# A two-layer hybrid encoder on one core: shift and scale rows summed together, x loaded through ScalarE's queue, and other buffers for the raw value weights, the lambda vectors and the bias table

## The chip, the cores and the metric

The kernel runs on one core of one Trainium2 chip. The metric is the device time of one execution in microseconds (us). The kernel is one program with one instruction stream for each engine: TensorE (PE in the profile), VectorE (DVE), ScalarE (ACT), GpSimd (POOL) and SyncE (SP). SP issues nearly all DMAs. The order of the instructions of each engine is fixed when the kernel is built; at run time an engine only waits, by semaphores, for what its next instruction needs.

## What is computed

Two layers, each with 512 tokens and 1024 channels in float32. Cut to what matters here:

```python
c_act = silu(c)
for l in range(2):
    shift, scale, gate = split(c_act @ w_ada[l] + b_ada[l])      # three rows of 1024
    h = rms_norm(x, g_pre[l]) * (1 + scale) + shift
    (cq, ckv, kr, za, qb, kb, vb, zb, qc, kc, vc, zc, gcols) = split_cols(h @ w_in[l])
    o_a = (mla_branch(cq, ckv, kr, ...) * silu(za)) @ w_o_mla[l]             # 8 heads
    o_b = (swa_branch(qb, kb, vb, sink[l], swa_bias) * silu(zb)) @ w_o_swa[l] # window 128, T5 bias
    lam = exp(sum(lam_q1 * lam_k1)) - exp(sum(lam_q2 * lam_k2)) + lam_init
    o_c = (diff_branch(qc, kc, vc, lam, g_sub, rel_bias) * silu(zc)) @ w_o_diff[l]
    g = sigmoid(gcols)                                            # 3 x 1024 gate columns
    y = (g[0] * o_a + g[1] * o_b + g[2] * o_c) @ w_out[l]
    x = x + gate * rms_norm(y, g_post[l])
```

The T5 bias of the windowed and the differential branch comes from a table of 32 x 12 numbers, spread over relative positions with a one-hot matrix.

## The kernel before

**Arithmetic.** Activations lie with channels on the partitions and tokens along the row ("hT", 8 tiles of 128 x 512). Nearly every product is made of three matmuls on a high and a low part of both operands (function `mm3`; L87, L88 and L89 are its three matmuls). So each raw weight tile is split first: ACT copies it to the high part (L81), DVE subtracts to get the low part (L84; POOL in a few places). One projection unit (`wunit`) takes one raw tile of 128 x 1024 ("wr") to "wh" and "wl" and then runs 24 matmuls of 512 columns into one tile of PSUM.

**Buffers.** A tile has a tag, and the tiles of a tag take its buffers in turn, in the order in which the program makes them. A tile waits until the tile that had its buffer before is done with. In SBUF: "wr" 2, "wh" 3, "wl" 3, "big" 8, "op" 12, "u" 8, "o" 4, "p" 2, "pt" 6, "tf" 2, "ta" 2. In PSUM: "dn" 2, "sc" 2, "tr" 2, "pj" 1, "av" 1. A waiting instruction holds up all that stand behind it on its engine.

**Order.** The tile framework orders the instructions of each engine when the kernel is built, by a simulated timeline with priorities (`tc.high_priority`) and with explicit "not before" relations (`behind`, `fence`). A tile that gets its buffer late in the program's order is therefore also placed late, and so is every tile behind it in the same tag's turn.

**Layer 0's start (`layer0_input`, L339).** `mod_load` (L143) brings columns of w_ada, `mod_chunk` (L187) makes from them one or two of the eight 128-wide pieces of shift and scale: DVE adds up eight 128 x 128 or 128 x 256 products for the shift and eight for the scale (L203, L206), PE sums over the partitions by a product with ones (L212), and DVE writes "ashf" and "amul" (L215 to L220). There are five chunks, for j = 0, 1, 2-3, 4-5 and 6-7; the scale of j = 1 is summed by PE itself (L194). `normed` scales the four tiles of x, PE transposes them into eight PSUM tiles (L346), ACT applies amul and ashf (L363) and makes the high part of hT, DVE the low part. For each j PE then adds the MLA input products (128 x 416, PSUM sc, sc, pj, av) and three tiles of za (128 x 512, PSUM dn, dn, tr). SP issues the loads of x behind those of the first chunk.

**After it (`rest_of_layer`, L1072).** The fourth tile of za ("z3"), norms and rotary parts (`mla_inputs`), the values (`mla_v`, L642), and the eight MLA heads (`mla_attention`), of which each has four score tiles (ps_sc), a maximum of each on DVE (L770), an exponential on ACT (L771), a scaling on POOL (L775), sixteen 128 x 128 transposes on PE (L704, ps_tr) and the product with the values (L713 to L717, ps_av). Then the program has `setup_bias` (L428): two matmuls (L438) of the one-hot matrix ("oh") into "dn" tiles, copied to "bt" and stored. Then the gate projections (`gates_early`), which take "dn" tiles too, the windowed branch, the differential branch and the merges. `setup_small` (L404) loads rotary tables and the lambda vectors and reduces the latter.

Of the kernel before, what the change touches and what calls it, by code (L numbers as in the profile page):

```python
# [50 lines left out]
def hybrid_kernel(ctx, tc, x, c, w_ada, b_ada, g_pre, g_post, w_in, g_q, w_uq, g_kv, w_ukv,  # L51
# [91 lines left out]
    def mod_load(l, j, n, tags):  # L143
        tags = iter(tags)
        res = []
        for which in range(2):
            raws = [T(next(tags), [P, KT // n, n * P]) for _ in range(n)]
            for i, raw in enumerate(raws):
                loads.append(sp.dma_start(out=raw, in_=w_ada[l].rearrange("(p k) b -> p k b", k=KT)
                             [:, i * (KT // n):(i + 1) * (KT // n),  # L150
                              which * D + j * P:which * D + (j + n) * P]))
            res.append([raws[k * n // KT][:, k % (KT // n)] for k in range(KT)])
# [12 lines left out]
    for t in range(NT):  # L165
        sp.dma_start(out=xt0[t], in_=x[t * P:(t + 1) * P, :])
# [20 lines left out]
    def mod_chunk(l, j, n, srcs, on_pe):  # L187
        pst = Q("tr")
        accs = []
        for which in range(2):  # L190
            src = srcs[which]
            if which in on_pe:
                for k in range(KT):
                    pe.matmul(pst[:, which * n:which * n + 1], src[k], cact[:, k:k + 1],  # L194
                              start=k == 0, stop=k == KT - 1)
                continue
            acc = T("o", [P, S])[:, 0:n * P]
            accs.append((which, src, acc))
        for k in range(KT):
            for which, src, acc in accs:  # L200
                with behind(*(stts if k < 4 else amuls)[-1:]) if stts else nullcontext():
                    if k == 0:
                        end = dve.tensor_scalar(out=acc, in0=src[0], scalar1=cact[:, 0:1],  # L203
                                                scalar2=None, op0=ALU.mult)
                    else:
                        end = dve.scalar_tensor_tensor(out=acc, in0=src[k],  # L206
                                                       scalar=cact[:, k:k + 1], in1=acc,
                                                       op0=ALU.mult, op1=ALU.add)
        stts.append(end)
        for which, src, acc in accs:  # L210
            for i in range(n):
                mm = pe.matmul(pst[:, which * n + i:which * n + i + 1],  # L212
                               acc[:, i * P:(i + 1) * P], ones[:, 0:1], start=True, stop=True)
        js = slice(j, j + n)
        dve.tensor_tensor(out=ashf[l][:, js], in0=pst[:, 0:n],  # L215
                          in1=par(l, PR_SHIFT, j, n), op=ALU.add)
        dve.scalar_tensor_tensor(out=amul[l][:, js], in0=pst[:, n:2 * n], scalar=1.0,
                                 in1=par(l, PR_SCALE, j, n),
                                 op0=ALU.add, op1=ALU.add)
        end = dve.tensor_tensor(out=amul[l][:, js], in0=amul[l][:, js],  # L220
                          in1=par(l, PR_GPRE, j, n), op=ALU.mult)
        sums.append(mm)
        amuls.append(end)
# [106 lines left out]
    def new_hT():  # L330
# [3 lines left out]
    AT = {0: (0,), 1: (1,), 2: (2,), 4: (3,)}  # L334
    CH = [(1, 1, ("wh", "wl"), (1,)),
          (2, 2, ("wh", "wl", "big", "big"), ()), (4, 2, ("big",) * 4, ()),
          (6, 2, ("big",) * 4, ())]

    def layer0_input():  # L339
        hh, hl = new_hT()  # L340
        mod_chunk(0, 0, 1, src0, ())
        xn = [normed(xt0[t]) for t in range(NT)]
        trs = [Q(g) for g in ("sc", "sc", "pj", "av", "dn", "dn", "tr", "tr")]
        for t in range(NT):
            for j in range(KT):
                pe.transpose(trs[j][:, t * P:(t + 1) * P], xn[t][:, j * P:(j + 1) * P], ident)  # L346
        xT = [T("op", [P, S]) for _ in range(KT)]
        for j in range(1, KT):
            act_copy(xT[j], trs[j])
        acc = acc4(True)  # L350
        zp = [Q("dn"), Q("dn"), Q("tr")]
        ws = mla_in_weights(0)
        for j in range(KT):
            w = next(ws)
            zr = T("tf", [P, S])[:, 0:ZK * P]
            zh = T("pt", [P, S], F32R)
            zl = T("pt", [P, S], F32R)
            sp.dma_start(out=zr, in_=w_in[0][j * P:(j + 1) * P, C_ZA:C_ZA + ZK * P])
            act_copy(zh[:, 0:ZK * P], zr)
            sub(zl[:, 0:ZK * P], zr, f(zh[:, 0:ZK * P]), pool)  # L360
            for i in AT.get(j, ()):
                mod_chunk(0, *CH[i][0:2], mod_load(0, *CH[i][0:3]), CH[i][3])
            act.activation(out=xT[j], in_=xT[j] if j else trs[0], func=AF.Identity,  # L363
                           scale=amul[0][:, j:j + 1], bias=ashf[0][:, j:j + 1])
            act_copy(hh[:, j], xT[j])
            sub(hl[:, j], xT[j], f(hh[:, j]))
# [61 lines left out]
    def setup_bias():  # L428
        oh = T("wr", [P, 1024])
# [5 lines left out]
        bt = T("wr", [P, 1024])  # L435
# [206 lines left out]
    def mla_v(l, cl):  # L642
        raw = T("wr", [P, 1024])
        h = T("wh", [P, 1024], F32R)
        sp.dma_start(out=raw, in_=w_ukv[l])
        rv = raw.rearrange("p (h b) -> p h b", h=8)[:, :, 64:128]
        hv = h[:, 0:512].rearrange("p (h b) -> p h b", h=8)
        lv = h[:, 512:1024].rearrange("p (h b) -> p h b", h=8)
        with behind():
            act_copy(hv, rv, par(l, PR_GKV))  # L650
            dve.scalar_tensor_tensor(out=lv, in0=rv, scalar=par(l, PR_GKV), in1=f(hv),
                                     op0=ALU.mult, op1=ALU.subtract)
# [417 lines left out]
    def rest_of_layer(l, hh, hl, acc, za):  # L1070
# [21 lines left out]
        if l == 0:  # L1092
            fence[:] = [amuls[2]]
# [45 lines left out]
        mb = merge_steps(l, 1, w_o_swa, ub, hh, hl, m, None)  # L1139
        od = diff_attention(l, hh, hl, lambda n: [next(mb) for _ in range(n)])  # L1140
# [79 lines left out]
```

## Time and profile before

| | |
|---|---|
| time, median of 3 | 1180.55 us (1180.5 to 1180.76) |
| the profiled execution's own time | 1178.78 us |
| its span | 1176.7 us |
| TensorE busy | 1146.0 us, 97% |
| VectorE busy | 844.2 us, 72% |
| ScalarE busy | 631.5 us, 54% |
| GpSimd busy | 181.3 us, 15% |
| mean granted TensorE clock | 0.993 |

The profile is of one execution. Its times count from the start of the span. "Busy" counts an instruction from its start to its end, and since instructions of one engine overlap in its pipeline, the distance between the starts of two neighbours (the step) is often shorter than the duration of one. In a timeline a row has the start, the duration, engine, line, operation, tiles, and in brackets the idle time ahead of it with what ended it. In a table of windows "(x)" counts instructions, PEclk is the clock that TensorE was granted, 1.00 being full.

### The profile page before, as it was taken

Reading aid. Unit: us, or ns where it says so; the run is one execution under the profiler, and the core shown is the slowest. Engines: PE = TensorE matmul, PEld = TensorE weight load, DVE = VectorE, ACT = ScalarE, POOL = GpSimd, SP = SyncE. Lnnn points to the kernel's source line nnn. Section 1 sums busy time; section 2 is a strip of 40 time slices with the busy share of each in tenths; the row PEclk is TensorE's granted clock in tenths of the full one; section 3 lists DMA queues with packets and bytes.
Section 4 is the critical chain, followed back from the end, with each engine's and each line's share of the span. In section 5 each row is a group of like instructions: output and inputs, shape, how many; then the busy total and the mean of one; then the engine's idle time right before and its main releaser. Section 6 shows DMA issues by size and latency. Waiting matters only on the chain.

```text
span 1176.7 us, 15536 instructions
## 1 busy us (share of the span) xinstructions
PE 1146.0 (97%) x5428; PEld 946.0 (80%) x5428; DVE 844.2 (72%) x1754; ACT 631.5 (54%) x1250; POOL 181.3 (15%) x226
## 2 busy tenths in 40 slices
PE   5899999999999999999999999999999999999997
PEld 4768788878887888888888888888888888888886
DVE  7956686898866687876577567688786568786654
ACT  5355464655543457664357456565564346675432
POOL 4310212122210010101211011222121001100120
PEclk9899999999999999999999999999999999999999
DMA  9537532256355433433454432324533333334442
GB/s 340 190 92 217 186 106 76 72 145 186 108 141 164 110 81 87 117 107 126 143 184 135 114 108 75 86 52 123 157 97 92 95 95 96 88 99 115 136 159 92
DMA packets 169522, 146.86 MB, mean 125 GB/s; under 512 B 7679, under 2 KB 146999, under 8 KB 169444
## 3 DMA queue, kind: packets, MB, share of 16 engines
q1 hardware_dynamic: 166148, 140.08, 40.9%
q10 hardware_dynamic: 3168, 5.77, 1.3%
q8 instruction: 43, 0.70, 0.2%
q14 instruction: 35, 0.29, 0.1%
q0 software_dynamic: 128, 0.01, 0.0%
HBM read 135.83 MB, written 14.20 MB: 127 GB/s over the span
## 4 chain that ended last, share of the span: by engine, by line
PE 84%; DVE 6%; DMA 3%; issue 3%; ACT 1%; POOL 1%; SPq 0%; DVEq 0%; POOLq 0%; ACTq 0%
PE ps_dn L87 20%; PE ps_dn L89 20%; PE ps_dn L88 19%; PE ps_tr L704 5%; PE ps_sc L89 2%; PE ps_sc L87 2%; PE ps_sc L88 2%; PE ps_av L714 1%; PE ps_av L713 1%; PE ps_sc L952 1%; PE ps_sc L953 1%; DMA wr<-in_w_in 1%; DVE o L206 1%; PE ps_pj L87 1%; PE ps_pj L88 1%
## 5 line engine op out<-in xcount | busy, mean ns | idle before, releaser
L87 PE MATMUL ps_dn<-hTh,wh 128*128 128x512 f32 x840 | 331.8, 395 | 1.4 <-DVE zz L479 0.8
L89 PE MATMUL ps_dn<-hTh,wl 128*128 128x512 f32 x840 | 330.5, 393 | 0.4 <-DVE wl L84 0.4
L88 PE MATMUL ps_dn<-hTl,wh 128*128 128x512 f32 x840 | 330.1, 393 | 0.0
L84 DVE TENSOR_TENSOR wl<-wr,wh 128x1024 fp32r<-128x1024 f32 x141 | 178.9, 1269 | 98.5 <-ACT wh L81 97.5
L81 ACT ACTIVATE wh<-wr 128x1024 fp32r<-128x1024 f32 x141 | 149.1, 1058 | 162.7 <-PE ps_dn L88 111.2
L87 PEld LDWEIGHTS ps_dn<-hTh,wh 128*128 128x128 f32 x840 | 158.2, 188 | 33.2 <-PE ps_dn L89 1.0
L89 PEld LDWEIGHTS ps_dn<-hTh,wl 128*128 128x128 f32 x840 | 158.0, 188 | 33.3 <-DVE wl L84 0.9
L88 PEld LDWEIGHTS ps_dn<-hTl,wh 128*128 128x128 f32 x840 | 158.1, 188 | 31.7
L84 DVE TENSOR_TENSOR pt<-ps_tr,pt 128x512 fp32r<-128x512 f32 x136 | 92.2, 684 | 30.5 <-ACT pt L81 29.6
L81 ACT ACTIVATE pt<-ps_tr 128x512 fp32r<-128x512 f32 x136 | 78.8, 596 | 64.8 <-PE ps_tr L704 63.6
L775 POOL TENSOR_SCALAR p<-p,st 128x512 f32<-128x512 f32 x64 | 52.2, 834 | 279.3 <-DVE st L773 243.7
L704 PE MATMUL ps_tr<-ident,p 128*128 128x128 f32 x544 | 92.4, 273 | 0.9 <-POOL p L775 0.6
L704 PEld LDWEIGHTS ps_tr<-ident,p 128*128 128x128 f32 x544 | 69.5, 141 | 20.2 <-POOL p L775 1.8
L87 PE MATMUL ps_dn<-u,wh 128*128 128x512 f32 x192 | 75.9, 395 | 0.0
L89 PE MATMUL ps_dn<-u,wl 128*128 128x512 f32 x192 | 75.9, 395 | 0.0
L88 PE MATMUL ps_dn<-u,wh 128*128 128x512 f32 x192 | 75.2, 391 | 0.0
L963 POOL TENSOR_SCALAR ta<-ta,st 128x512 f32<-128x512 f32 x32 | 26.7, 834 | 306.9 <-ACT wh L81 143.1
L894 POOL TENSOR_SCALAR p<-p,st 128x256 f32<-128x256 f32 (+1 forms) x64 | 42.1, 676 | 157.7 <-DVE st L892 130.4
L771 ACT ACTIVATE p<-ps_sc,st 128x512 f32<-128x512 f32 x64 | 43.7, 685 | 28.0 <-DVE st L770 27.7
L770 DVE TENSOR_REDUCE st<-ps_sc 128x1 f32<-128x512 f32 x64 | 43.4, 686 | 21.3 <-PE ps_sc L89 20.8
L886 ACT ACTIVATE p<-p,st 128x256 f32<-128x256 f32 (+1 forms) x64 | 35.7, 558 | 21.9 <-DVE st L884 21.2
L959 ACT ACTIVATE p<-p,st 128x512 f32<-128x512 f32 x32 | 23.1, 723 | 38.8 <-DVE st L957 38.7
(345 smaller groups left out, 2100.5 us busy)
## 6 DMA issues: line engine op xcount, KB each, us to landing
wr<-in_w_in SPq DMA_DIRECT2D x105, 512.0 KB, 3.7
wr<-in_w_ada SPq DMA_DIRECT2D x32, 512.0 KB, 3.6
wr<-in_w_out SPq DMA_DIRECT2D x16, 512.0 KB, 3.6
big<-in_w_ada SPq DMA_DIRECT2D x10, 512.0 KB, 7.6
big<-in_x SPq DMA_DIRECT2D x8, 512.0 KB, 5.3
wr<-in_w_o_mla SPq DMA_DIRECT2D x8, 512.0 KB, 4.0
wr<-in_w_o_swa SPq DMA_DIRECT2D x8, 512.0 KB, 3.4
wr<-in_w_o_diff SPq DMA_DIRECT2D x8, 512.0 KB, 3.7
```

The costliest lines, as they stand in the source:

```text
L81: return act.activation(out=out_, in_=in_, func=AF.Copy, scale=scale)
L84: return (eng or dve).tensor_tensor(out=out_, in0=a, in1=b, op=ALU.subtract)
L87: pe.matmul(o, ah, bh, start=start, stop=False)
L88: pe.matmul(o, ah, bl, start=False, stop=False)
L89: pe.matmul(o, al, bh, start=False, stop=stop)
L704: pe.transpose(tr[:, i * P:(i + 1) * P], b, ident)
L770: dve.tensor_reduce(out=nm[:, t:t + 1], in_=s, axis=AX.X, op=ALU.max, negate=True)
L771: act.activation(out=pr[:, t], in_=s, func=AF.Exp, bias=nm[:, t:t + 1], accum_out=sm[:, t:t + 1])
L775: pool.tensor_scalar(out=pr[:, t], in0=pr[:, t], scalar1=rr[:, t:t + 1], scalar2=1.0, op0=ALU.mult, op1=ALU.mult)
L886: act.activation(out=pr[:, i, :w], in_=pr[:, i, :w], func=AF.Exp, bias=nm[:, i:i + 1], accum_out=sm[:, i:i + 1])
L894: pool.tensor_scalar(out=pr[:, i, :w], in0=pr[:, i, :w], scalar1=rr[:, i:i + 1], scalar2=1.0, op0=ALU.mult, op1=ALU.mult)
L963: pool.tensor_scalar(out=pc[1], in0=pc[1], scalar1=rr[:, 1:2], scalar2=1.0, op0=ALU.mult, op1=ALU.mult)
```

## The change

- `mod_load` puts shift and scale of one k side by side in one tile, and `mod_chunk` sums them together: eight DVE steps of 128 x 256 (n = 1) or 128 x 512 (n = 2) instead of sixteen of half the width. PE no longer sums the scale of j = 1. What follows the sums has a priority raised by 200. The last chunk is split into j = 6 and j = 7, the last issued at step j = 5.
- x is loaded by ACT's queue, at the start of the program, and no longer by SP.
- The transposes of x go through PSUM in three groups (dn, dn, tr) instead of eight tiles at once.
- `setup_lam` is split off `setup_small`, and moved behind the creation of the windowed branch's merge in layer 0; its tile has the tag "ta" instead of "tf".
- `setup_bias` has its one-hot matrix and its table in one tile of the tag "p" (the probabilities' buffers) instead of two of "wr".
- `mla_v` loads its weights in two halves of the tag "op" instead of one "wr".
- The weights of the MLA heads in layer 0 wait for the last amul instead of the third (`fence[:] = [amuls[2]]` is gone).

```diff
     def mod_load(l, j, n, tags):
...
+        for i, tag in enumerate(tags):
+            raw = T(tag, [P, ks, 2, n * P])
+            for which in range(2):
+                loads.append(sp.dma_start(out=raw[:, :, which],
...
     xt0 = [T("big", [P, D]) for _ in range(NT)]
+    for t in range(NT):
+        act.dma_start(out=xt0[t], in_=x[t * P:(t + 1) * P, :])
...
-    for t in range(NT):
-        sp.dma_start(out=xt0[t], in_=x[t * P:(t + 1) * P, :])
...
+        acc = T("o", [P, S])[:, 0:2 * n * P]
         for k in range(KT):
+            with behind(*(stts if k < 2 else amuls)[-1:]) if stts else nullcontext():
+                if k == 0:
+                    end = dve.tensor_scalar(out=acc, in0=src[0], scalar1=cact[:, 0:1],
...
+        with tc.high_priority(offset=200):
+            for i in range(2 * n):
+                mm = pe.matmul(pst[:, i:i + 1], acc[:, i * P:(i + 1) * P], ones[:, 0:1],
+                               start=True, stop=True)
...
-    AT = {0: (0,), 1: (1,), 2: (2,), 4: (3,)}
+    AT = {0: (0,), 1: (1,), 2: (2,), 4: (3,), 5: (4,)}
+    CH = [(1, 1, ("wh", "wl")), (2, 2, ("wh", "wl", "big", "big")), (4, 2, ("big",) * 4),
+          (6, 1, ("big",) * 2), (7, 1, ("big",) * 2)]
...
-        trs = [Q(g) for g in ("sc", "sc", "pj", "av", "dn", "dn", "tr", "tr")]
+        for js in ((0, 1, 2), (3, 4, 5), (6, 7)):
+            trs = {j: Q(g) for j, g in zip(js, ("dn", "dn", "tr"))}
...
+    def setup_lam():
         for l in range(DEPTH):
-            lt = T("tf", [P, 4, 64])
+            lt = T("ta", [P, 4, 64])
...
     def setup_bias():
-        oh = T("wr", [P, 1024])
+        room = T("p", [P, NT, S]).rearrange("p (a b) c -> p a (b c)", a=2)
+        oh, bt = room[:, 0], room[:, 1]
...
-        bt = T("wr", [P, 1024])
...
     def mla_v(l, cl):
-        raw = T("wr", [P, 1024])
         h = T("wh", [P, 1024], F32R)
-        sp.dma_start(out=raw, in_=w_ukv[l])
+        for i in range(2):
+            raw = T("op", [P, S])
+            sp.dma_start(out=raw, in_=w_ukv[l][:, i * S:(i + 1) * S])
...
-        if l == 0:
-            fence[:] = [amuls[2]]
         wts = {0: mla_pair_weights(l, 0, "ta")}
...
         mb = merge_steps(l, 1, w_o_swa, ub, hh, hl, m, None)
+        if l == 0:
+            setup_lam()
```

**TensorE in the middle of layer 0's MLA attention.** In these rows, and in those below, "ps_dn" from "hTh" or "hTl" with "wh" or "wl" is a projection of hT, "ps_av" the product of probabilities and values, "ps_sc" scores, "ps_tr" transposes of probabilities; a name ahead of the shape is output<-inputs. Before:

```order
L89 MATMUL ps_dn_2016<-hTh_120,wl_2012 128x512
L87 MATMUL ps_dn_2016<-hTh_120,wh_2011 128x512
L713 MATMUL ps_av_1066<-pt_1072,big_866 128x512
L88 MATMUL ps_dn_2016<-hTl_121,wh_2011 128x512
L89 MATMUL ps_dn_2016<-hTh_120,wl_2012 128x512
L87 MATMUL ps_sc_1055<-op_892,op_938 128x512
L88 MATMUL ps_sc_1055<-op_893,op_938 128x512
L89 MATMUL ps_sc_1055<-op_892,op_939 128x512
L714 MATMUL ps_av_1066<-pt_1073,big_866 64x512
```

The same stretch in the changed kernel:

```order
L88 MATMUL ps_sc_1102<-op_950,op_984 128x512
L89 MATMUL ps_sc_1102<-op_949,op_985 128x512
L715 MATMUL ps_av_1030<-pt_1036,big_830 128x512
L716 MATMUL ps_av_1030<-pt_1037,big_830 64x512
L715 MATMUL ps_av_1030<-pt_1047,big_837 128x512
L706 MATMUL ps_tr_1053<-ident_73,p_916 128x128 x4
L716 MATMUL ps_av_1030<-pt_1048,big_837 64x512
L706 MATMUL ps_tr_1064<-ident_73,p_916 128x128 x4
L715 MATMUL ps_av_1030<-pt_1058,big_844 128x512
```

The projection products that stood between the steps of the heads are gone from here; from the end of z3 to the last head the changed order has none of them, and before there were 17 units of 24 matmuls between the heads' steps.

**TensorE at the bias table.** The two products of the one-hot matrix (L438 before, L439 after) into "dn" tiles stood before among those of z3 (ps_dn_686), ahead of all heads:

```order
L88 MATMUL ps_dn_686<-hTl_121,wh_681 128x512
L89 MATMUL ps_dn_686<-hTh_120,wl_682 128x512
L438 MATMUL ps_dn_1774<-wr_1767,rb_1769 12x512
L630 MATMUL ps_tr_766<-ident_73,ta_749 128x128 x3
L631 MATMUL ps_tr_766<-ident_73,ta_749 64x128
L87 MATMUL ps_dn_686<-hTh_120,wh_681 128x512
```

In the changed kernel they stand in the last head, and the first gate unit (ps_dn_1752) follows them:

```order
L719 MATMUL ps_av_1635<-pt_1674,big_851 128x512
L706 MATMUL ps_tr_1695<-ident_73,p_1602 128x128 x3
L439 MATMUL ps_dn_1737<-p_1731,rb_1733 12x512
L439 MATMUL ps_dn_1740<-p_1731,rb_1733 12x511
L706 MATMUL ps_tr_1684<-ident_73,p_1602 128x128
L706 MATMUL ps_tr_1695<-ident_73,p_1602 128x128
L87 MATMUL ps_dn_1752<-hTh_122,wh_1747 128x512
```

The one-hot matrix (p_1731) now has a buffer of the probabilities, of the seventh head (p_1521), and so the two "dn" tiles come late; the gates' "dn" tiles come behind them in the tag's turn.

**ScalarE at the input of j = 4 and 5.** In layer 0's input stage, before, where L363 applies amul and ashf to xT of j = 4 and 5 (op_222, op_223):

```order
L81 ACTIVATE pt_442<-tf_441 128x384
L363 ACTIVATE op_222<-op_222,ashf_7_69,amul_5_67 128x512
L363 ACTIVATE op_223<-op_223,ashf_7_69,amul_5_67 128x512
L81 ACTIVATE hTh_120<-op_222 128x512
L81 ACTIVATE hTh_120<-op_223 128x512
L81 ACTIVATE wh_681<-wr_680 128x1024
```

In the changed kernel (op_175, op_176, L362):

```order
L81 ACTIVATE wh_641<-wr_640 128x1024
L81 ACTIVATE wh_817<-op_818,prT_25_114 128x256
L81 ACTIVATE pt_420<-tf_419 128x384
L362 ACTIVATE op_175<-op_175,ashf_7_69,amul_5_67 128x512
L362 ACTIVATE op_176<-op_176,ashf_7_69,amul_5_67 128x512
L81 ACTIVATE hTh_122<-op_175 128x512
L81 ACTIVATE hTh_122<-op_176 128x512
```

The copies of z3's weights (wh_641) and of half the value weights (wh_817) moved ahead of the step of j = 4.

More of the change, by code (lines that the diff above doesn't have):

```diff
@@ L185, in hybrid_kernel, with mod_chunk @@
     stts, amuls, sums = [], [], []
-    def mod_chunk(l, j, n, srcs, on_pe):
+    def mod_chunk(l, j, n, src):
         pst = Q("tr")
[L189 to L198, printed above, removed]
-        for k in range(KT):
[L200 to L208, printed above, removed]
-        stts.append(end)
[L210 to L221, printed above, removed]
@@ new lines, in mod_chunk @@
+        acc = T("o", [P, S])[:, 0:2 * n * P]
+        for k in range(KT):
+            with behind(*(stts if k < 2 else amuls)[-1:]) if stts else nullcontext():
+                if k == 0:
+                    end = dve.tensor_scalar(out=acc, in0=src[0], scalar1=cact[:, 0:1],
+                                            scalar2=None, op0=ALU.mult)
+                else:
+                    end = dve.scalar_tensor_tensor(out=acc, in0=src[k],
+                                                   scalar=cact[:, k:k + 1], in1=acc,
+                                                   op0=ALU.mult, op1=ALU.add)
@@ L361, in layer0_input @@
             for i in AT.get(j, ()):
[L362 to L366, printed above, removed]
+                mod_chunk(0, *CH[i][0:2], mod_load(0, *CH[i]))
+            if j > 0:
+                act.activation(out=xT[j], in_=xT[j], func=AF.Identity,
+                               scale=amul[0][:, j:j + 1], bias=ashf[0][:, j:j + 1])
+                act_copy(hh[:, j], xT[j])
+                sub(hl[:, j], xT[j], f(hh[:, j]))
             mla_in_step(acc, w, j, hh, hl)
```

55 lines of the change are left out of this document (32 added, 23 removed).

## Prediction

> **What bounds the kernel now.** I read the page first: the span, the busy times and the shares of the chain that ended last.
>
> ```profile
> span 1176.7 us, 15536 instructions
> PE 1146.0 (97%) x5428; PEld 946.0 (80%) x5428; DVE 844.2 (72%) x1754; ACT 631.5 (54%) x1250; POOL 181.3 (15%) x226
> PE 84%; DVE 6%; DMA 3%; issue 3%; ACT 1%; POOL 1%; SPq 0%; DVEq 0%; POOLq 0%; ACTq 0%
> ```
>
> TensorE is busy for 97% and has 84% of the chain. All its idle time is 30.7 us (1176.7 less 1146.0); that is the most that a better order can win, and any stretch in which TensorE lacks work costs its full length. So I read next where TensorE idles, by windows:
>
> ```profile
> core 0: us, PE busy (x) PEld busy (x) DVE busy (x) ACT busy (x) POOL busy (x), PEclk, DMA share, GB/s
> 0.00:10.00 10.00, 0.28 (x1) 0.18 (x1) 4.54 (x22) 2.56 (x4) 2.98 (x10) 1.00 0.76 256
> 10.00:20.00 10.00, 6.91 (x36) 5.62 (x37) 7.86 (x22) 6.89 (x15) 5.79 (x7) 1.00 1.08 380
> 20.00:30.00 10.00, 9.24 (x47) 8.37 (x46) 9.72 (x21) 6.51 (x13) 4.66 (x4) 0.83 1.08 387
> 30.00:40.00 10.00, 7.62 (x28) 6.36 (x28) 9.75 (x22) 3.50 (x7) 2.94 (x4) 0.71 1.04 350
> 40.00:50.00 10.00, 9.79 (x49) 8.61 (x47) 9.86 (x21) 2.60 (x9) 4.24 (x3) 0.94 0.46 147
> 50.00:60.00 10.00, 7.27 (x40) 6.86 (x41) 7.67 (x20) 6.54 (x11) 3.62 (x3) 1.00 0.18 54
> 80.00:90.00 10.00, 9.24 (x43) 7.05 (x43) 6.25 (x15) 5.26 (x13) 0.00 (x0) 1.00 0.77 203
> 90.00:130.00 40.00, 40.00 (x178) 32.97 (x177) 26.72 (x48) 20.07 (x39) 0.59 (x1) 1.00 0.73 217
> 130.00:150.00 20.00, 19.28 (x95) 15.32 (x94) 11.56 (x17) 10.16 (x23) 5.85 (x8) 1.00 0.43 138
> 230.00:250.00 20.00, 17.86 (x94) 14.09 (x93) 19.47 (x37) 10.37 (x20) 4.41 (x4) 0.98 0.57 156
> ```
>
> Two things. Most idle time lies in the first 60 us, where the DMA engines are full to 40 us (350 to 387 GB/s, 13.7 MB) and VectorE is full from 20 to 50. And layer 0's MLA attention, from 90 us on, keeps TensorE at 40.00 of 40.00 us, although VectorE has only 26.72 us of work there: the gate projections between the heads' steps fill it.
>
> **The input stage.** TensorE's timeline, at the four places that matter, and VectorE's at the last chunks:
>
> ```profile
> 21.06 1.95 PE L194 MATMUL ps_tr<-cact,wl 128*128 128x1 f32 x16 [0.76 <-ACT op L81]
> 23.09 0.44 PE L87 MATMUL ps_sc<-u,hTh 128*128 128x416 f32 x1
> 34.23 0.99 PE L212 MATMUL ps_tr<-ones,o 128*128 128x1 f32 x4 [2.38 <-DVE o L206]
> 52.73 0.46 PE L87 MATMUL ps_sc<-u,hTh 128*128 128x416 f32 x1 [2.94 <-ACT hTh L81]
> 73.18 0.50 PE L87 MATMUL ps_dn<-hTh,wh 128*128 128x512 f32 x1 [0.78 <-DVE zz L479]
> ...
> 9.59 0.34 DVE L206 SCALAR_TENSOR_TENSOR o<-wh,cact,o 128x128 f32<-128x128 f32 x1
> 9.86 0.73 DVE L206 SCALAR_TENSOR_TENSOR o<-wl,cact,o 128x128 f32<-128x128 f32 x2
> 50.44 0.16 DVE L220 TENSOR_TENSOR amul<-amul,prT 128x2 f32<-128x2 f32 x1
> 50.52 2.85 DVE L206 SCALAR_TENSOR_TENSOR o<-big,cact,o 128x256 f32<-128x256 f32 x7
> 53.29 0.68 DVE L84 TENSOR_TENSOR hTl<-op,hTh 128x512 fp32r<-128x512 f32 x1
> 53.90 0.47 DVE L206 SCALAR_TENSOR_TENSOR o<-big,cact,o 128x256 f32<-128x256 f32 x1
> 54.29 0.68 DVE L84 TENSOR_TENSOR hTl<-op,hTh 128x512 fp32r<-128x512 f32 x1
> ```
>
> The joint sums: a step is 0.26 us at 128 columns (9.59 to the next at 9.86), 0.39 at 256 (53.90 to 54.29) and 0.61 at 512 (53.29 to 53.90). Before there are 24 steps of 128 columns and 48 of 256, 25.0 us; now 32 of 256 and 16 of 512, 22.2 us. That wins only 2.8 us; what counts more is that j = 4, 5 no longer shares VectorE with the last chunk, whose first steps stood ahead of amul at 50.44. By the changed order I put this amul at 41 us, just behind the last of its 13.7 MB, which no queue can bring sooner than the full windows did. ScalarE has three weight copies ahead of it, whose loads land at about 40 too, so hTh of j = 4 comes at 44. TensorE begins at 20 instead of 23.09 (the 1.95 us of L194 and its wait are gone), needs 24 to 25 us for j = 0 to 3 (26.6 before, less the wait of 2.38), and comes to j = 4 at 45. From j = 4 to z3 it took 20.45 us (52.73 to 73.18), of which some 17.3 are work at full clock: z3 begins at 62.5, **a gain of 10.7 us**. Bounds: 14 with j = 4 at 41.5 and no wait, 5 with ScalarE held up by one of the three loads until 50.
>
> The rule in the Trainium skill, "DMA: Bandwidth & Descriptors", section "Issuing engines are not separate DMA queues", speaks against the move of x: transfers of all issuers run on the same 16 DMA engines, and a second issuer saves only issue time. The full windows to 40 us agree, and I count nothing for the move.
>
> **MLA attention without fillers.** Since the one-hot matrix now waits for a buffer of the probabilities, the bias table's two "dn" tiles come in the last head, and all gate projections stand behind them. TensorE's order from z3 to there has 248 matmuls and 136 transposes. A matmul costs 0.225 us (40.00 us by 178, in the window 90:130), a transpose 0.11:
>
> ```profile
> 17.76 0.27 PE L346 MATMUL ps_pj<-ident,big 128*128 128x128 f32 x1
> 17.87 0.27 PE L346 MATMUL ps_av<-ident,big 128*128 128x128 f32 x1
> ```
>
> 55.8, 15.0 and 1 for the rest make 71.8 us: alone, TensorE would end at 134.3. But VectorE sets the pace:
>
> ```profile
> 68.85 0.37 ACT L612 ACTIVATE ta<-ps_sc 128x256 f32<-128x256 f32 x1
> 77.25 0.72 DVE L682 SCALAR_TENSOR_TENSOR x<-pt,prT,x 128x192 fp32r<-128x192 f32 x3
> 84.46 1.22 DVE L84 TENSOR_TENSOR wl<-wr,wh 128x1024 fp32r<-128x1024 f32 x1 [1.90 <-ACT wh L81]
> 88.24 1.23 DVE L84 TENSOR_TENSOR wl<-wr,wh 128x1024 fp32r<-128x1024 f32 x1 [1.37 <-ACT wh L81]
> 91.45 0.41 DVE L741 CAST op<-kp 64x512 fp32r<-64x512 f32 x1
> L770 DVE TENSOR_REDUCE st<-ps_sc 128x1 f32<-128x512 f32 x32 | 21.8, 687 | 15.4 <-PE ps_sc L89 15.0
> ```
>
> The norms and values take 22.6 us before (68.85 to 91.45), 19.3 without the two waits for weight copies (1.90 and 1.37). They begin 4.3 us ahead of z3, so at 58.2 now, and end between 77.5 and 80.8; I take 79.5, and 82 with the first head's k and q. Then VectorE has, by the changed order, 92 operations 512 wide (a step of 0.61: 56.1 us), 12 casts of 0.41 (4.9), three weight preparations of seven narrow operations (three take 0.72, so 1.7 each, 5.1) and, an estimate, eight reciprocals of 0.1: 66.9 us. To these come waits, since the last exponential, the reciprocal and the scaling of a head leave little to do. The last row, VectorE's group of maxima in the heads, bounds them: 15.4 us of idle before 32 of them, for scores that stood behind fillers; below by nothing. I take 7, the middle. That ends at 155.9, and 1.5, an estimate, for the one-hot matrix's load gives 157.4 for the first gate. TensorE has thus **23.1 us more idle time** (157.4 less 134.3). Bounds: 12.7 (80.1 and 66.9, no waits) and 32.5 (83.4, 66.9, 15 and 1.5). What goes against it: the 3.6 us that TensorE idles between 80 and 250 now (0.76, 0.72 and 2.14) mostly go, since all 17 gate units stand in what follows; I take 3, with bounds 0 and 3.6.
>
> **The clock.** Windows of 3.40 us around two gaps:
>
> ```profile
> 30.90:34.30 3.40, 1.01 (x9) 0.93 (x7) 3.26 (x6) 0.00 (x0) 0.91 (x1) 1.00 1.06 374
> 34.30:37.70 3.40, 3.40 (x10) 2.91 (x11) 3.29 (x12) 1.20 (x3) 0.00 (x0) 0.50 0.99 324
> ...
> 246.00:249.40 3.40, 1.39 (x6) 0.84 (x6) 3.34 (x10) 0.76 (x1) 0.00 (x0) 0.99 0.97 244
> 249.40:252.80 3.40, 3.40 (x11) 2.63 (x10) 3.34 (x8) 3.07 (x8) 0.00 (x0) 0.51 0.24 64
> ```
>
> Behind windows that were 30% and 41% busy (1.01 and 1.39 of 3.40) the granted clock was half. TensorE would be about 75% busy without fillers, so one or two windows may fall under the mark: 1.7 us each, I take 2, between 0 and 6.
>
> The Trainium skill, "TensorE: Matmul & The Clock Gate", section "What's actually happening", has the gate close after an idle window of some 3.4 us. The window of 1.39 us busy says that it needn't be idle; by the page the sum would be without the 2.
>
> **The other edits** I put at 0. The lambda vectors now load later, under work that TensorE bounds; uncovered, they would cost the some 2 us that VectorE and ScalarE spend on them. The bias table's stores come later by some 80 us, but five gate units with weights already split (27 us at 24 matmuls each) stand between. Half-width value weights have the same bytes and ScalarE columns. The weights of the heads that wait for the last amul have the 19.3 us of norms as cover.
>
> **Sum.** -10.7 + 23.1 + 2 - 3 = +11.4. The profiled execution took 1178.78 (span and 2.1 around it), so 1190.2; the median of 3 is 1.8 higher, which gives **1192.0**.
>
> **Rivals.**
> 1. *Faster:* VectorE runs the unfilled heads without waits, idle 12.7, and the input stage wins all of 14: -14 + 12.7 - 3 = -4.3, **1176.3**. It decides on whether VectorE's waits stay under some 3 us in the eight heads. For it speaks that in the window 230:250 VectorE is busy 19.47 of 20; against it the 15.4 us of waits for scores, and that "pj" and "av" have one buffer each.
> 2. *The input stage doesn't get shorter as meant:* ScalarE stands behind a late load, and the gain is 5: -5 + 23.1 + 2 - 3 = +17.1, **1197.7**. For it speaks the full DMA to 40 us.
> 3. *The clock:* many windows of the unfilled stretch fall to half, 14 of them at 1.7 us: 24 instead of 2, +33.4, **1214.0**. Only if busy time comes in bursts. It is also what the Trainium skill, "TensorE: Matmul & The Clock Gate", section "A second HAM failure mode: psum-queue depth-cycling", describes: short idle times between groups that make the clock swing. The windows 230:250 (0.98) speak against much of it.
> 4. *Nothing much:* the fillers lost and the input stage won cancel to within 2.4 us.
>
> **How the numbers follow.** About 0.2%, 2.4 us, is what a measurement of this kernel can tell from no change. Forecast 0.60 (1184 to 1202), rival 1 0.15, of which 0.03 within 0.2%, rival 2 0.13, rival 3 0.06, the fourth 0.06, of which 0.01 faster. So faster 0.13, same 0.08, slower 0.79. The range runs from 1176 (rival 1) to 1207 (gain 5, idle 32.5, clock 2, recovered 3: +26.5); rival 3 is left out.
>
> **What the profile will show.** Right: z3's first product at about 62, no projection of hT from there to about 157, VectorE over 85% busy and TensorE about 75% between 82 and 156, and TensorE full behind it to 250. Wrong: fillers between the heads, or a TensorE that is over 90% busy without them; z3 not before 68; windows of half clock by the dozen.

## The result and the profile after

| | before | changed |
|---|---|---|
| median of 4 | 1180.65 us (1180.5 to 1180.77) | 1219.66 us (1217.43 to 1219.9) |
| span of the profiled execution | 1176.7 | 1217.8 |
| TensorE busy | 1146.0 | 1161.7 |

The changed kernel takes 1.0327 times as long, 95% interval 1.031 to 1.0343: 39 us slower. Forecast were 1192.0, with 1207 as the upper end. From the page of the changed kernel, the same three lines as before:

```profile
span 1217.8 us, 15537 instructions
PE 1161.7 (95%) x5414; PEld 948.9 (78%) x5414; DVE 842.0 (69%) x1735; ACT 632.9 (52%) x1252; POOL 179.0 (15%) x226
PE 80%; DVE 8%; DMA 6%; ACT 2%; issue 2%; POOL 1%; SPq 0%; DVEq 0%; POOLq 0%; ACTq 0%
```

TensorE's idle time is 56.1 us instead of 30.7. Its timeline of the changed kernel at the places that the prediction named (start, duration, line, tiles, in brackets the idle time ahead):

```profile
40.00 0.71 PE L87 MATMUL ps_sc<-u,hTh 128*128 128x416 f32 x1 [1.34 <-ACT hTh L81]
51.60 0.46 PE L87 MATMUL ps_sc<-u,hTh 128*128 128x416 f32 x1 [0.43 <-ACT hTh L81]
70.93 0.50 PE L87 MATMUL ps_dn<-hTh,wh 128*128 128x512 f32 x1 [0.48 <-DVE st L302]
98.98 0.63 PE L87 MATMUL ps_sc<-op,op 128*128 128x512 f32 x1
181.63 1.88 PE L439 MATMUL ps_dn<-p,rb 33*12 33x512 f32 x4
183.63 0.48 PE L87 MATMUL ps_dn<-hTh,wh 128*128 128x512 f32 x1
```

These are the beginnings of j = 2, of j = 4 and of z3, the first score of the heads, the bias table and the first gate. z3 is 2.25 us sooner than before (73.18), not 10.7, and the first gate comes at 183.63, not 157.4. Windows of the changed kernel, three of the input stage and three that go from the first norm to the end of the heads:

```profile
core 0: us, PE busy (x) PEld busy (x) DVE busy (x) ACT busy (x) POOL busy (x), PEclk, DMA share, GB/s
20.00:30.00 10.00, 9.16 (x51) 8.41 (x50) 9.72 (x17) 8.34 (x17) 4.02 (x4) 1.00 1.04 354
30.00:40.00 10.00, 6.06 (x28) 4.46 (x26) 9.79 (x11) 3.67 (x8) 7.86 (x6) 0.81 1.08 325
40.00:50.00 10.00, 10.00 (x46) 9.29 (x47) 5.02 (x13) 2.84 (x5) 1.01 (x1) 0.85 0.85 251
...
98.98:181.60 82.62, 71.11 (x316) 50.48 (x314) 66.72 (x123) 53.17 (x126) 22.91 (x32) 0.93 0.02 6
87.27:98.98 11.71, 6.29 (x15) 4.00 (x14) 6.17 (x11) 3.24 (x5) 0.00 (x0) 0.50 0.23 63
68.53:87.27 18.74, 13.78 (x63) 9.72 (x62) 14.36 (x59) 14.75 (x55) 2.78 (x4) 1.00 0.21 60
```

From the last norm to the first score (87.27 to 98.98) no engine is busy throughout, and TensorE runs at half clock (0.50). In the heads VectorE is busy 66.72 of 82.62 us, TensorE 71.11, part of it at half clock.

A measure for what follows: "lost" time of TensorE, worked out from windows of 3.41 us over the whole span, is the idle time plus busy time times (1 less the granted clock).

| lost us, idle / half clock | before | changed |
|---|---|---|
| 0 to 80 | 20.4 / 5.1 | 22.8 / 2.7 |
| 80 to 180 | 1.2 / 0.0 | 19.5 / 8.7 |
| 180 to the end | 9.2 / 1.6 | 13.8 / 3.1 |

In these sums nothing at all is won in the input stage (25.5 us lost before and now), 27 us are lost where the fillers were, and 6 behind. The other 8 of the 41 us of span are in busy time at full clock. A matmul counts as busy for 0.39 us on average, while in a row of them the next starts after 0.23, so a short break can leave a tail that counts as busy; that this makes up the 8 us is not shown.

### The profile page after: what moved, and what is told of

Its sections match the earlier page's. It is cut to its first block, busy times and chain, and to the rows that moved or that the text cites. A ratio compares the mean times of both kernels' runs of the same rounds, so it can differ in the third digit from the quotient of the medians.

```text
span 1217.8 us, 15537 instructions
## 1 busy us (share of the span) xinstructions
PE 1161.7 (95%) x5414; PEld 948.9 (78%) x5414; DVE 842.0 (69%) x1735; ACT 632.9 (52%) x1252; POOL 179.0 (15%) x226
## 4 chain that ended last, share of the span: by engine, by line
PE 80%; DVE 8%; DMA 6%; ACT 2%; issue 2%; POOL 1%; SPq 0%; DVEq 0%; POOLq 0%; ACTq 0%
PE ps_dn L87 18%; PE ps_dn L88 18%; PE ps_dn L89 18%; PE ps_tr L706 4%; PE ps_sc L87 2%; PE ps_sc L88 2%; PE ps_sc L89 2%; DMA wr<-in_w_in 1%; PE ps_pj L87 1%; PE ps_sc L954 1%; PE ps_sc L955 1%; DMA wr<-in_w_ada 1%; PE ps_pj L88 1%; PE ps_pj L89 1%; PE ps_av L716 1%
## 5 line engine op out<-in xcount | busy, mean ns | idle before, releaser
L777 POOL TENSOR_SCALAR p<-p,st 128x512 f32<-128x512 f32 x64 | 49.7, 796 | 223.1 <-DVE st L775 177.4
L773 ACT ACTIVATE p<-ps_sc,st 128x512 f32<-128x512 f32 x64 | 43.8, 686 | 26.8 <-DVE st L772 26.4
L772 DVE TENSOR_REDUCE st<-ps_sc 128x1 f32<-128x512 f32 x64 | 43.3, 684 | 13.8 <-PE ps_sc L89 12.5
L81 ACT ACTIVATE op<-ps_dn 64x512 fp32r<-64x512 f32 (+1 forms) x57 | 33.4, 589 | 23.9 <-DVE op L809 18.7
```

What stands on the lines that cost most here:

```text
L81: return act.activation(out=out_, in_=in_, func=AF.Copy, scale=scale)
L772: dve.tensor_reduce(out=nm[:, t:t + 1], in_=s, axis=AX.X, op=ALU.max, negate=True)
L773: act.activation(out=pr[:, t], in_=s, func=AF.Exp, bias=nm[:, t:t + 1], accum_out=sm[:, t:t + 1])
L777: pool.tensor_scalar(out=pr[:, t], in0=pr[:, t], scalar1=rr[:, t:t + 1], scalar2=1.0, op0=ALU.mult, op1=ALU.mult)
```

## The experiments

Theory: the gates, which the bias table holds up, leave layer 0's MLA heads to VectorE's pace; this is nearly the whole loss. Rivals: another part of the change costs as well, or the clock does. Ratios are to the kernel before, run beside each.

### The bias table

Undone in the changed kernel (e1_bias_wr), half undone (e2_bias_pj), and alone in the kernel before (e3_before_p, which makes the opposite edit of the first):

```diff
# e1_bias_wr
-        room = T("p", [P, NT, S]).rearrange("p (a b) c -> p a (b c)", a=2)
-        oh, bt = room[:, 0], room[:, 1]
+        oh = T("wr", [P, 1024])
...
+        bt = T("wr", [P, 1024])
# e2_bias_pj
-            pb = Q("dn")
+            pb = Q("pj")
```

> The changed kernel with one part undone: the one-hot matrix and the table in two buffers of wr again, so that the bias table's two dn tiles come ahead of the heads and the gate projections stand between the heads' steps. Theory A (the lost fillers are the loss, and the rest of the change moves only z3, 2.25 us sooner): 1178 to 1183 us, no idle gap of TensorE over 1 us from 80 to 180, no window at half clock there. Rival B (the joint sums, held up by GpSimd, or another part of the change costs as well): 1190 or more. Rival C (in between): the fillers return but the weights' split and the heads compete for VectorE: 1184 to 1190.

> The changed kernel with one word changed: the table's two PSUM tiles have the tag pj instead of dn; the one-hot matrix still waits for a buffer of the probabilities. Theory A (the turn of the dn tiles is what moves the gates): as the kernel with wr, 1178 to 1184. Rival B (the late buffer of the probabilities is itself the cost, since the table and the windowed branch's bias come late): over 1195, with a wait of the windowed branch for its bias.

> The kernel before with one part of the change alone: one-hot matrix and table in one tile of the tag p. Theory A: nearly all of the 39 us, 1212 to 1224, with gaps and half clock in the heads as in the changed kernel. Rival B (the loss needs the other parts too): 1181 to 1200.

| | median us | ratio, 95% interval |
|---|---|---|
| e1_bias_wr | 1185.87 | 1.0063 [1.0048, 1.0078] |
| e2_bias_pj | 1196.82 | 1.0155 [1.014, 1.017] |
| e3_before_p | 1218.74 | 1.0344 [1.0329, 1.036] |

This one part alone makes the kernel before as slow as the changed one, as theory A of e3_before_p had it, and undone in the changed kernel it gives back 33.8 of the 39 us. The parts don't simply add up: with the bias table undone the rest of the change costs 7.1 us (against 1178.79 for the kernel before in the same round), and on top of the bias table nothing that can be seen. In e1_bias_wr the heads are filled again; the window of its trace that before showed 40.00:

```profile
90.00:130.00 40.00, 39.29 (x175) 32.17 (x174) 27.91 (x50) 20.56 (x41) 0.00 (x0) 1.00 0.63 193
```

e2_bias_pj tells the turn of the dn tiles from the late buffer. With the matrix as late as in the change, but its products in another tag, the gates come back and 22.8 us with them; 11 stay lost against e1_bias_wr. Two places in its trace show these: a window in which the fillers have run out and heads are left, and, later, ScalarE, TensorE and VectorE behind the bias stores that SP issues from 250 to 266 (the windowed branch waits for its bias x<-bs, the next weights for their load):

```profile
200.00:220.00 20.00, 15.06 (x66) 9.92 (x65) 18.50 (x30) 11.00 (x23) 4.17 (x4) 0.91 0.38 106
...
265.38 1.06 ACT L81 ACTIVATE wh<-wr 128x1024 fp32r<-128x1024 f32 x1 [6.86 <-DMA wr<-in_w_in]
268.34 0.80 PE L87 MATMUL ps_dn<-hTh,wh 128*128 128x512 f32 x1 [3.00 <-DVE zz L480]
273.31 0.48 DVE L882 CUSTOM_DVE_ANT_0 p<-ps_sc,x,sinkt 128x256 f32<-128x256 f32 x1 [4.42 <-DMA x<-bs]
```

So both theories of that run hold in part (the time and the wait for the bias are rival B's): the turn of the dn tiles is two thirds of the loss. The other third goes with the late table, or with the pj buffer that its products take in this run; that was not separated. e1_bias_wr is in the range of its rival C, still slower than before, so the rest of the change costs too; its reason, a competition for VectorE in the heads, was not tested.

### What sets the pace of the unfilled heads

e7_dummies gives TensorE more to do there; e11_no_plow takes work from VectorE (it leaves out the low part of the probabilities in layer 0's MLA heads; TensorE's products stay, with the high part in its place).

```diff
# e7_dummies: in first(h) of mla_attention
+            if l == 0:
+                idle = Q("dn")
+                for i in range(8):
+                    pe.matmul(idle, onesr, qh, start=True, stop=True)
# e11_no_plow: in transposed_block, for layer 0's MLA
+        if not low:
+            return ph, ph
         pl = T("pt", [P, S], F32R)
         sub(pl, tr, f(ph))
```

> The changed kernel with 64 products more (8 behind the scores of each of layer 0's MLA heads, onto a dn tile that nothing reads; 14.5 us at full clock). Nothing of the result changes. Theory A (TensorE waits in this stage, and short of work its clock falls): the products fit into gaps and keep the clock up, no window at half clock between 105 and 180 (three before), time 1213 to 1220. Rival B (TensorE's order is what the stage waits for, so more work is more time): 1229 to 1236. Rival C: in blocks of 8 they delay the transposes, and part of them shows: 1221 to 1228.

> The changed kernel without the low part of the probabilities in layer 0's MLA heads (the high part stands in its place, TensorE has the same products): 32 operations of 0.61 us less on VectorE in these heads, 19.5 us. Theory A (VectorE sets the pace of the unfilled heads): the way from the first score to the first gate falls by 12 to 19 us from 84.7, time 1201 to 1208. Rival B (the chain through TensorE, ScalarE and GpSimd with its single buffers sets it): by less than 6, time 1214 to 1220.

e7_dummies took 1220.1 us (1.0347 [1.0331, 1.0362]), e11_no_plow 1205.86 (1.023 [1.0215, 1.0244]). A window in the heads of the changed kernel, the same of e7_dummies, and the heads of e11_no_plow:

```profile
105.00:180.00 75.00, 64.72 (x294) 46.50 (x294) 61.13 (x110) 48.60 (x112) 21.71 (x31) 0.93 0.02 5
...
105.00:180.00 75.00, 70.08 (x345) 52.40 (x343) 59.29 (x108) 48.05 (x112) 19.89 (x29) 1.00 0.02 5
...
97.09:166.60 69.51, 63.02 (x316) 47.52 (x315) 49.98 (x96) 53.02 (x126) 21.84 (x32) 0.98 0.03 8
```

With 14.5 us of products more TensorE's clock is whole (1.00 instead of 0.93), as theory A had it. The time is the same, at the upper edge of its range, and the way from the first score to the first gate is 1.5 us longer (86.14 us, from 98.33 to 184.47, against 84.65): TensorE's work does not set the pace there. What the whole clock may have won and what the products may have cost were not measured apart. In e11_no_plow VectorE is busy 49.98 us in the heads instead of 66.72; the way from the first score to the first gate falls from 84.65 to 71.5 us (97.09 to 168.62) and the time by 13.8, as its theory A had it: VectorE's work sets the pace. One thing that this edit does not separate: the subtraction that it leaves out is also a link between the transposes and the product with the values, so the chain of each head gets shorter too.

### The input stage

e4_input_only is the kernel before with the new input stage alone. The others start from e1_bias_wr: e5_v_wr undoes `mla_v` too, e6_no_pool takes GpSimd's subtractions out of the stage (it leaves out the low parts of these weights), e8_x_sp loads x by SP.

```diff
# e4_input_only against the changed kernel: setup_lam inside setup_small again, bias table and
# value weights in wr, fence[:] = [amuls[2]] back
# e5_v_wr
-        for i in range(2):
-            raw = T("op", [P, S])
+        raw = T("wr", [P, 1024])
# e6_no_pool, and the like in mla_in_weights
-            sub(zl[:, 0:ZK * P], zr, f(zh[:, 0:ZK * P]), pool)
+            act_copy(zl[:, 0:ZK * P], zr)
# e8_x_sp
-        act.dma_start(out=xt0[t], in_=x[t * P:(t + 1) * P, :])
+        sp.dma_start(out=xt0[t], in_=x[t * P:(t + 1) * P, :])
```

> The kernel before with the input stage of the change alone: x by ScalarE's queue, joint sums, transposes in three groups, last chunk split; lambda vectors, bias table, value weights and the heads' fence as before. Theory A: z3 at 70 to 72 us instead of 73.18, time 1177 to 1181. Rival B (the wide sums lose more to GpSimd than they save): z3 at 74 or later and 1182 or more.

> The kernel with the bias table in wr again (1185.87 us), and the raw value weights in one buffer of wr again too. In both kernels with halves in op TensorE idles about 2.2 us more at layer 1's values, between 600 and 700 us, and 0.4 without. Theory A (that is the only place where they count): 1183.5 to 1185. Rival B (the buffers of wr are short in the input stage, as in the kernel with the input stage alone): 1187 to 1195, lost before 100 us.

> The kernel with the bias table in wr again, and GpSimd's subtractions in layer 0's input stage replaced by copies of the whole raw weight on ScalarE: the low parts of these weights are left out (they hold the raw weight instead). Theory A (VectorE's wide steps wait for GpSimd's instructions, and this holds the sums for j = 2, 3 and so all that follows): a step of 512 columns takes 0.6 to 0.75 us throughout, amul of j = 2, 3 by 34 instead of 37.2, z3 at 64 to 67 instead of 70.7, time 1178 to 1183. Rival B (the loads alone limit the stage): steps are short but wait for data, amul of j = 2, 3 at 36 or later, z3 at 69 or later, time 1184 or more.

> The kernel with the bias table in wr again, and x loaded by SP behind the first chunk's weights, as before. Theory A (the DMA engines are full either way, and the queue that issues x doesn't matter): 1185 to 1187, z3 within 1 us of 70.7. Rival B (x ahead of the first weights holds up the sums): z3 sooner by 1 to 3 us and 1182 to 1185. Rival C (ScalarE's queue frees SP for the loads behind): z3 later and 1187 to 1190.

| | median us | ratio, 95% interval | z3 at |
|---|---|---|---|
| e4_input_only | 1194.68 | 1.0137 [1.012, 1.0154] | 77.39 |
| e1_bias_wr | 1185.87 | 1.0063 [1.0048, 1.0078] | 70.72 |
| e5_v_wr | 1182.74 | 1.0026 [1.0012, 1.004] | 69.53 |
| e6_no_pool | 1177.14 | 0.9989 [0.9976, 1.0003] | 65.12 |
| e8_x_sp | 1185.91 | 1.0056 [1.0041, 1.0071] | 73.35 |

e4_input_only has the late z3 and the time of rival B, but its trace names another reason than the wide sums. GpSimd, VectorE and TensorE in its trace:

```profile
58.74 1.11 POOL L84 TENSOR_TENSOR pt<-tf,pt 128x384 fp32r<-128x384 f32 x1 [1.74 <-ACT pt L81]
...
66.99 0.22 DVE L414 TENSOR_TENSOR tf<-tf 128x64 f32<-128x64 f32 x1 [0.95 <-DMA tf<-in_lam_q]
68.12 0.21 DVE L419 TENSOR_SCALAR lamc<-st 128x1 f32<-128x1 f32 x1
68.25 0.15 DVE L211 TENSOR_TENSOR amul<-amul,prT 128x1 f32<-128x1 f32 x1
...
69.97 0.72 PE L87 MATMUL ps_sc<-u,hTh 128*128 128x416 f32 x1 [5.37 <-ACT hTh L81]
```

The lambda vectors' tile has the tag "tf" here, and so it waits for a buffer that holds za's weights until GpSimd has subtracted them (58.74 and 1.11 more). The vectors therefore load late, they stand ahead of the last amul on VectorE, and TensorE waits 5.37 us. By this trace the new input stage needs the move of `setup_lam` to another tag and place (the e1 kernel, which has it, doesn't wait there), but no run makes this move alone. The wait is also not all of the loss: against the kernel before, TensorE loses 6.9 us more between 60 and 80, and 6.5 more between 200 and 300, whose cause is open.

e6_no_pool shows what holds the joint sums. VectorE's steps and GpSimd's subtractions in the changed kernel:

```profile
22.80 1.31 DVE L197 SCALAR_TENSOR_TENSOR o<-wl,cact,o 128x256 f32<-128x256 f32 x1
24.03 1.31 DVE L194 TENSOR_SCALAR o<-wh,cact 128x512 f32<-128x512 f32 x1
25.38 1.37 DVE L197 SCALAR_TENSOR_TENSOR o<-wh,cact,o 128x512 f32<-128x512 f32 x1
29.84 4.46 DVE L197 SCALAR_TENSOR_TENSOR o<-big,cact,o 128x512 f32<-128x512 f32 x3
...
22.67 2.38 POOL L84 TENSOR_TENSOR p<-wr,u 128x416 fp32r<-128x416 f32 x2 [4.69 <-ACT u L81]
29.50 2.84 POOL L84 TENSOR_TENSOR p<-wr,u 128x416 fp32r<-128x416 f32 x2 [3.31 <-ACT u L81]
```

The same steps in e6_no_pool:

```profile
22.12 0.48 DVE L194 TENSOR_SCALAR o<-wh,cact 128x512 f32<-128x512 f32 x1
22.64 0.75 DVE L197 SCALAR_TENSOR_TENSOR o<-wh,cact,o 128x512 f32<-128x512 f32 x1
...
28.68 2.32 DVE L197 SCALAR_TENSOR_TENSOR o<-big,cact,o 128x512 f32<-128x512 f32 x3
```

While GpSimd subtracts, a step of VectorE takes 1.3 to 1.5 us whether it is 256 or 512 columns wide, about as long as one subtraction (2.38 and 2.84 for two). Without it the two-input step (L197) takes 0.75 at 512 columns and the first step of a sum (L194) 0.48. amul of j = 2, 3 comes at 32.4 instead of 37.35 in e1_bias_wr, z3 5.6 us sooner, and the time is 8.7 less: theory A, for the sums and z3. The time falls by 3.1 us more than z3; where these come from is open. The Trainium skill, "SBUF — State Buffer", section "SBUF: two separate sides", says that a VectorE instruction with two inputs in SBUF and a GpSimd instruction that reads SBUF share a pair of ports, which the one that begins first holds for its whole length. The L197 rows agree (1.31 us at 256 columns, 1.37 at 512); the L194 step, with one tile as input, is held up as well (1.31), and these words don't cover it.

e8_x_sp: the queue of x moves z3 by 2.6 us and the time not at all (the time of theory A, z3 as in rival C). In e5_v_wr the time is 3.1 us less, below the ranges of both its theories, so the halves do cost. Where is less clear. TensorE's lost time over the whole span is 38.2 us there and 43.8 in e1_bias_wr; from 20 to 100 us it is 10.0 and 13.1, and from 600 to 700, at layer 1's values, 1.3 and 2.2. So theory A's place is a small part, and the input stage the larger, but 2.2 of its 3.1 us are half clock. z3 is 1.2 us sooner, and that alone says little: in the changed kernel, e7_dummies and e11_no_plow, which have the same input stage, z3 begins at 70.93, 69.99 and 69.98. What keeps e5_v_wr 3.2 us behind the kernel before in its round (1179.55) was not split further.

### Versions

With that, GpSimd's subtractions were to be moved in two ways on e5_v_wr, and in the first way in the kernel before:

```diff
# e9_subs_dve on e5_v_wr, e12_before_subs_dve on the kernel before; the like in mla_in_weights
-            sub(zl[:, 0:ZK * P], zr, f(zh[:, 0:ZK * P]), pool)
+            sub(zl[:, 0:ZK * P], zr, f(zh[:, 0:ZK * P]))
# e10_subs_late on e5_v_wr
+            with behind(amuls[-1]) if j >= 2 else nullcontext():
                 sub(zl[:, 0:ZK * P], zr, f(zh[:, 0:ZK * P]), pool)
```

> Base: the changed kernel with the bias table and the value weights in wr again (1182.74 us). Edit: GpSimd's subtractions in layer 0's input stage done by VectorE, so that the result is complete. Theory A (what a GpSimd subtraction costs VectorE, up to a whole instruction of 1.2 to 1.4 us for each of VectorE's, is more than the subtraction takes on VectorE itself, 0.5): amul of j = 2, 3 at 34 to 36 instead of 37.3, z3 at 66 to 69 instead of 69.5, time 1178 to 1181. Rival B (VectorE is full to 44 us, and 24 operations more outweigh it): z3 at 70 or later, 1183 to 1188.

> Same base. Edit: GpSimd's subtractions for j = 2 and later may not start ahead of the last amul that is known there, so those of j = 2, 3 come behind the sums of j = 2, 3. Theory A (they only stand in the way of these sums): amul of j = 2, 3 at 33 to 35, time 1178 to 1181. Rival B (TensorE then waits for the low parts, and the next sums are held up instead): 1183 to 1190.

> The kernel before with GpSimd's subtractions in layer 0's input stage done by VectorE. Theory A (as above; VectorE lost about 11 us to GpSimd there, and gets 24 operations of 0.4 to 0.5 us): z3 at 71 to 73, time 1177 to 1180. Rival B (the operations stand on VectorE where it is full): z3 at 75 or later, 1182 or more.

| | median us | ratio, 95% interval | amul of j = 2, 3 at | z3 at |
|---|---|---|---|---|
| e9_subs_dve | 1182.29 | 1.0021 [1.0013, 1.003] | 35.50 | 67.92 |
| e10_subs_late | 1181.71 | 1.0019 [1.001, 1.0029] | 37.51 | 69.65 |
| e12_before_subs_dve | 1174.55 | 0.9968 [0.9955, 0.9982] | 33.97 | 68.36 |

In e10_subs_late the subtractions did not move: GpSimd begins those of j = 2, 3 at 30.06, against 29.89 in e5_v_wr, and amul isn't sooner (37.51 and 37.33). The edit did not do what it was meant to, and its theories stay untested. In e9_subs_dve amul and z3 come sooner as expected, but the time doesn't follow (1182.29, between the ranges of its two theories): up to 60 us TensorE loses 0.9 us less than in e5_v_wr (19.5 and 20.4), and behind it 1.9 more, in small places. In the kernel before the same edit wins 5 us by the medians (0.3%, interval 0.18% to 0.45%), more than its theory A forecast, and **it is faster than both kernels**. Why it pays there and not on e5_v_wr is open. VectorE and TensorE there (36.31 and 73.18 before):

```profile
33.97 0.16 DVE L220 TENSOR_TENSOR amul<-amul,prT 128x2 f32<-128x2 f32 x1
68.36 0.50 PE L87 MATMUL ps_dn<-hTh,wh 128*128 128x512 f32 x1 [0.21 <-DVE zz L479]
```

## Why the prediction was right in kind and wrong in size

| step | forecast | measured |
|---|---|---|
| first norm begins | 58.2 | 68.53 |
| norms and values | 21.3 us | 18.74 us |
| k and q of the first head | 2.5 us | 11.71 us |
| first score to first gate | 75.4 us | 84.65 us |
| first gate | 157.4 | 183.63 |

- **The mechanism was right.** The gates follow the bias table and the heads are left without fillers (e1_bias_wr, e3_before_p); that the change is slower was forecast at 0.79. The first gate is 26.2 us later than forecast, and the time missed 1192.0 by 27.7, so nearly all of the error lies ahead of the first gate.
- **The step that failed by most is "23.1 us more idle time", the pace of the unfilled heads and what leads up to them.** With the prediction's own 71.8 us of work for TensorE from z3 on (70.93 and 71.8 make 142.7), a first gate at 183.63 makes this term 40.9, beyond its upper bound of 32.5. Of the 17.8 us more, 9.2 are the k and q of the first head, 9.25 the heads, and 1.9 the norms' start, which is 2.4 us ahead of z3 and not 4.3; the norms themselves took 2.6 less.
- **Input stage: "a gain of 10.7 us" measured 2.25**, below its lower bound of 5. j = 4 begins at 51.60 and not at 45 (6.6 us), and z3 comes 19.3 after it and not 17.5. (45 and 17.3 make 62.3; the prediction wrote 62.5.) It failed at "I put this amul at 41 us, just behind the last of its 13.7 MB". The sums for j = 4, 5 were done at 43.4, but TensorE's addition over the partitions stood in its queue behind the products of j = 2 and 3, which began only at 40.00, since their own amul came at 37.2. TensorE's addition and VectorE in the changed kernel:

```profile
48.06 0.95 PE L203 MATMUL ps_tr<-ones,o 128*128 128x1 f32 x8
...
41.89 1.53 DVE L197 SCALAR_TENSOR_TENSOR o<-big,cact,o 128x512 f32<-128x512 f32 x2
49.05 0.16 DVE L206 TENSOR_TENSOR ashf<-ps_tr,prT 128x2 f32<-128x2 f32 x1 [4.84 <-PE ps_tr L203]
```

  What held the amul of j = 2, 3 was GpSimd (e6_no_pool). The prediction took VectorE's steps at their price without it, and left GpSimd's subtractions out of this stage; in the changed kernel they keep GpSimd busy for 7.86 us between 30 and 40. The prediction also passed a gain at z3 on to the time one for one. The runs don't bear this out in general: between e1_bias_wr and e8_x_sp z3 differs by 2.6 us and the time not at all, and e9_subs_dve has z3 1.6 sooner than e5_v_wr for 0.5 us.
- **k and q of the first head: 2.5 forecast, 11.71 measured.** There is one pj buffer, so the k of the pair must be read by ScalarE and VectorE before q's products begin, and then each step waits for the one before. VectorE comes to the last read of k only at 91.74, because it works nearly without a break from 87.27 on, with casts for the keys and a weight of 1.23 us among its work. In the changed kernel:

```profile
88.40 1.23 DVE L84 TENSOR_TENSOR wl<-wr,wh 128x1024 fp32r<-128x1024 f32 x1 [0.27 <-ACT wh L81]
91.74 0.69 DVE L84 TENSOR_TENSOR op<-ps_pj,op 64x512 fp32r<-64x512 f32 x1
...
92.58 0.77 PE L87 MATMUL ps_pj<-big,x 128*128 128x512 f32 x1 [4.64 <-DVE op L84]
95.51 0.69 DVE L755 TENSOR_TENSOR ta<-ps_pj,rq 128x512 f32<-128x512 f32 x1 [3.08 <-PE ps_pj L89]
96.24 0.63 ACT L81 ACTIVATE op<-ta 128x512 fp32r<-128x512 f32 x1 [4.79 <-DVE ta L755]
96.90 0.69 DVE L84 TENSOR_TENSOR op<-ta,op 128x512 fp32r<-128x512 f32 x1 [0.69 <-ACT op L81]
101.29 0.69 DVE L772 TENSOR_REDUCE st<-ps_sc 128x1 f32<-128x512 f32 x1 [0.73 <-PE ps_sc L89]
```

  The prediction counted 2.5 us for this step, and not its chain. TensorE is at half clock here (0.50); whether full clock would shorten this chain was not tried.
- **The heads.** VectorE's work, 66.9 us from the order of its instructions, is measured as 66.72: right. Its waits were taken as 7, with 15.4 as the upper end; measured is 82.62 less 66.72, 15.9. VectorE's waits in the heads of the changed kernel (for what, us in total, how often, the longest):

```profile
DVE st L772 <- PE ps_sc L89: 6.3, 10, 1.1
DVE pt L84 <- ACT pt L81: 2.9, 5, 0.9
DVE ta L755 <- PE ps_pj L89: 2.7, 2, 1.6
```

  That the upper end meets the measured size is luck: it was taken from waits for scores behind fillers, and of the waits here only 6.3 us are for scores; the rest is for ScalarE, GpSimd and the next head's q. The step's main claim, that VectorE sets the pace, is borne out by e11_no_plow, with the reservation made there. Two small terms had no row behind them: the eight reciprocals take 0.17 us each and not 0.1, and the 1.5 us for the one-hot matrix's load compare with 2.4 from its issue at 179.25 to its first product.
- **The clock, +2 and the rival of +24.** Half clock took 8.7 us from 80 to 180, 4.2 of them at the k and q and 4.5 in the heads. In the heads e7_dummies, with a whole clock and more products, is no faster.
- **"The 3.6 us mostly go".** Lost time of TensorE from 180 us on is 16.9 instead of 10.8: it grew by 6, and the cause is open.
- **"The other edits at 0".** The queue of x: right for the time. The value weights in halves cost 3.1 us. The lambda vectors' move spares the new input stage a wait of 5.37 us by the trace of e4_input_only; no run measured it alone.
- **The rivals.** The second (input gain of 5) was right that the input stage hardly gets shorter, but not in its reason: in the changed kernel ScalarE was ready for j = 4 at 44.65 and waited 4.86 us for amul, not for a load. The third, 1214.0, is nearest in number, and by luck: it counted 24 us of half clock, where 8.7 were measured. No rival took late k and q into account.
- **The signs.** z3 not before 68 was named as a sign of being wrong, and it came (70.93). In the heads VectorE was busy for 81% (over 85% forecast) and TensorE for 86% (about 75%).

## What to carry to other kernels

A buffer that comes late makes everything late that stands behind it in the turn of another tag: when a tile moves to another pool, follow its consumers' PSUM tags to the work that filled TensorE. Between two stages count the chain through single buffers step by step, since the sum of each engine's work does not give it. Where VectorE is the limit, look at what GpSimd does at the same time before pricing VectorE's steps.

## What the runs showed of the hardware

Beside GpSimd's subtractions (1.19 to 1.42 us each) VectorE's step of a sum took about as long as one of them at either width: 1.31 us at 256 columns, 1.37 and 1.49 at 512. Without them it took 0.47 at 256 (the prediction's rows) and 0.75 at 512. The clock fell after windows that were not idle, and it stayed down through one that was 77% busy at half clock; four windows of the changed kernel, the last two behind one another:

```profile
128.27:131.68 3.41, 1.69 (x8) 0.91 (x7) 3.31 (x8) 2.62 (x8) 1.85 (x3) 1.00 0.10 31
131.68:135.09 3.41, 3.09 (x9) 2.08 (x8) 3.35 (x10) 1.85 (x6) 1.01 (x2) 0.51 0.00 0
...
94.17:97.58 3.41, 2.63 (x7) 1.62 (x6) 1.37 (x2) 0.63 (x1) 0.00 (x0) 0.50 0.00 0
97.58:100.99 3.41, 3.41 (x9) 2.63 (x9) 1.35 (x5) 1.77 (x7) 0.00 (x0) 0.50 0.00 0
```

The first was busy for 1.69 of 3.41 us at full clock, and the next had 0.51.
